# One core, a streaming encoder step: where the products with the expert weights are made, how many gathered rows run beside them, how the weights are put away, and how many v tiles are multiplied unsplit

## The chip, the core and the metric

The kernel runs on one core of one Trainium2 chip. The core has TensorE (PE, with the loading of its weights shown as PEld), VectorE (DVE), ScalarE (ACT), GpSimd (POOL), SyncE (SP, which here only issues transfers) and 16 DMA engines. The metric is the device time of one execution in microseconds (us). Before the change the median of 3 runs is 1786.55 us (1782.0 to 1789.22).

## The reference

One layer is computed for 384 tokens: 8 sequences of 16 tokens (the samples) and one prompt of 256 tokens. The layer has a modulation, an RWKV branch, a sparse attention branch, a mix, and then PEER, a layer with 16,384 experts. Only PEER is touched here:

```
q = (hb @ w_pq).reshape(PEER_BLOCK, PEER_HEADS, 2, PEER_DHALF)
s = jnp.einsum('nhpd,hpkd->nhpk', q, peer_keys)
s1, i1 = lax.top_k(s[:, :, 0], PEER_TOPK)
s2, i2 = lax.top_k(s[:, :, 1], PEER_TOPK)
...
sc, j = lax.top_k(cand, PEER_TOPK)
e = jnp.take_along_axis(cidx, j, axis=-1)
g = jax.nn.softmax(sc, axis=-1)
act = jax.nn.gelu(jnp.einsum('nhkd,nd->nhk', peer_u[e], hb))
out = jnp.einsum('nhk,nhkd->nd', (g * act), peer_v[e])
```

Each token picks 8 x 16 = 128 experts; an expert has a row u and a row v of 1024 numbers each. All in 32-bit floats.

## The kernel before

**Two ways to PEER.** The 128 sample tokens are done sparsely: 128 times, one picked expert of each token is gathered by an indirect DMA (one *row*: 128 partitions x 2048 numbers, 1 MB, u and v beside each other). VectorE forms the dot product with u (L1567), ScalarE takes the gelu and the weight (L1568, L1569), VectorE adds the scaled v to the sum (L1573). Three buffers hold such rows. The 256 prompt tokens are done densely: all 16,384 experts, in 128 tiles of 128 experts. For tile j, `dense_u` multiplies u with the tokens and takes the gelu, giving an activation tile of 128 experts x 256 tokens; this is multiplied by the matrix of routing weights, which is zero for experts not picked; `dense_v` multiplies the product with v and adds it to four PSUM banks (`bx`, `cp` for the first 128 tokens, two of `dx` for the second).

**Kept and late tiles.** Tiles 0 to 75 are *kept*: their activations stay in SBUF (G1 and G2) before the routing weights exist. Tiles 76 to 127 are *late*: their activations are computed later (`gA`) or put to HBM and fetched again (`gO`, `gB`).

**The stages.** (1) `dense_u` for the kept tiles, the first 36 unsplit. (2) The weights stage: `weights` goes over the 256 tokens in 64 steps of 4. A step makes two one-hot factors `oh` (L1384 on VectorE; L1432 on VectorE or L1436 and L1437 on ScalarE), multiplies them on TensorE into a PSUM tile p of 4 tokens x 128 tiles, multiplies the 76 kept columns into G1 and G2 (L1397, two instructions, 36 and 40 columns), and copies the 52 late columns to `wst` (L1398), which after 8 steps goes to HBM (L1400): the put-away weights. In odd steps ScalarE first copies the kept columns to `wg` (L1394, two buffers) and GpSimd makes the product; in even steps VectorE makes it straight from PSUM. After each step `ahead` is called: half of the times it runs a `dense_u` of a late tile, 31 in all, and it pulls rows at a rate `SR[1]`. (3) The v stage: 128 times a `dense_v`, kept and late tiles interleaved, with 21 more `dense_u` and rows at a rate `SR[2]`. Late weights are fetched for four tiles at a time (`Ws`, L1530) and multiplied on GpSimd (L1495). (4) The last two tiles and the residuals.

**Whole and split.** A number is cut into a high and a low part so that TensorE can use its faster mode (names ending in h and l: `wh`, `wl`, `Gh`, `Gl`). A *split* v tile costs a copy on ScalarE (L230) and a subtraction on VectorE (L234) for v and for G, and 12 matmuls of 512 columns. A *whole* tile needs none of that and 4 matmuls in full precision, which the trace shows as 8. `VN` says which are whole: the first three, and from the 9th to the 107th every n that VN divides.

**What sets the order.** The program is recorded in the order of the code, and a scheduler then orders each engine's instructions by a simulated time line; each engine runs its own list in order. Rows therefore run earlier or later than the place at which they were pulled. All plain transfers are issued by SP, in its order, each when its buffer is free; row gathers are issued by GpSimd in its own order, between its products. A row in the v stage is also held until a v tile five places before it is done (`pace`).

## Time and profile before

| | |
|---|---|
| median of 3 runs | 1786.55 us |
| profiled execution | 1789.7 us |
| its span | 1787.9 us |
| mean granted TensorE clock | 0.978 |
| PE, DVE, ACT, POOL busy, share of the span | 95%, 77%, 42%, 31% |
| HBM read, written | 403.23 MB, 31.30 MB |

The span is the time from the first to the last instruction; the execution's own time has 1.8 us around it. Busy times of an engine don't count waiting. A view "by stretches" gives, for a stretch of the span, the busy time of each engine with the number of instructions, the granted clock, the share of time in which the 16 DMA engines were busy, and the rate. The weights stage is the stretch from 1165 to 1305 us (ten of its 64 steps run some of their work before it), the v stage that from 1305 to 1758 us.

### The profile page before, as it was taken

What the parts mean: (1) busy time and instruction counts of PE and PEld (TensorE: products, weight loads), DVE (VectorE), ACT (ScalarE), POOL (GpSimd) and SP (SyncE); (2) the same over time, 40 slices, a digit from 0 to 9 for tenths busy, and PEclk for the clock granted to TensorE, in tenths of its full rate; (3) what the DMA queues carried; (4) which work ended last, traced back from release to release, by engine and by line L of the source; (5) the groups of instructions that cost most, each with busy time, mean ns of one, the idle gap of its engine ahead of it and who ended that gap; (6) DMA issues with size and microseconds to landing.
All of it is one profiled execution on the core that took longest, in us unless ns stands there. A gap on an engine that the chain in (4) does not pass through costs nothing.

```text
span 1787.9 us, 33229 instructions
## 1 busy us (share of the span) xinstructions
PE 1695.1 (95%) x12424; PEld 1414.2 (79%) x12424; DVE 1368.0 (77%) x2925; ACT 754.4 (42%) x1647; POOL 556.7 (31%) x648
## 2 busy tenths in 40 slices
PE   6999999999999998999999999999998989999998
PEld 4987788878888876998788789999976666666666
DVE  4538787777867765455999998899957877888787
ACT  4533333333243333334323365579833433334344
POOL 2423243333332320034032232333342324233232
PEclk8999899999999998999999999999999999999999
DMA  9443662454364365665498989975589989999995
GB/s 319 150 121 92 195 191 73 145 166 146 95 208 141 104 219 203 202 199 176 131 349 328 347 303 375 367 239 178 186 316 369 354 332 388 388 359 372 382 371 190
DMA packets 172537, 436.71 MB, mean 244 GB/s; under 512 B 46036, under 2 KB 86100, under 8 KB 155992
## 3 DMA queue, kind: packets, MB, share of 16 engines
q1 hardware_dynamic: 153944, 300.36, 49.9%
q0 software_dynamic: 18432, 134.23, 19.8%
q8 instruction: 98, 1.61, 0.4%
q14 instruction: 63, 0.52, 0.1%
HBM read 403.23 MB, written 31.30 MB: 243 GB/s over the span
## 4 chain that ended last, share of the span: by engine, by line
PE 55%; DVE 19%; DMA 13%; issue 7%; ACT 3%; POOL 2%; SPq 1%; DVEq 0%; POOLq 0%; ACTq 0%
PE mm L226 21%; PE fx L226 13%; PE dx L226 8%; PE cp L226 6%; PE bx L226 5%; DMA w<-in_pv 4%; DVE wl L234 3%; DMA w<-in_puT 3%; DVE raw L1567 3%; DVE acc L1573 2%; DMA raw<-in_puv,pe 2%; ACT wh L230 1%; DMA d<-MBp 1%; DMA NL<-d 1%; DMA w<-in_w_ada 1%
## 5 line engine op out<-in xcount | busy, mean ns | idle before, releaser
L234 DVE TENSOR_TENSOR wl<-w,wh 128x1024 fp32r<-128x1024 f32 (+1 forms) x280 | 352.8, 1265 | 121.2 <-ACT wh L230 80.2
L230 ACT ACTIVATE wh<-w 128x1024 fp32r<-128x1024 f32 (+1 forms) x288 | 301.1, 1052 | 195.0 <-PE mm L226 83.9
L1560 POOL DMA_INDIRECT raw<-in_puv,pe x128 | 169.3, 1323 | 438.8 <-PE dx L226 128.3
L226 PE MATMUL fx<-h2h,wl 128*128 128x256 f32 x736 | 210.5, 286 | 9.5 <-DVE wl L234 9.3
L226 PE MATMUL fx<-h2h,wh 128*128 128x256 f32 x736 | 212.9, 289 | 5.0 <-ACT wh L230 3.0
L226 PE MATMUL fx<-h2l,wh 128*128 128x256 f32 x736 | 207.6, 282 | 0.0
L1573 DVE SCALAR_TENSOR_TENSOR acc<-raw,dots,acc 128x1024 f32<-128x1024 f32 x127 | 166.5, 1311 | 18.3 <-ACT dots L1569 18.1
L1567 DVE SCALAR_TENSOR_TENSOR raw<-raw,sh 128x1024 f32<-128x1024 f32 x128 | 157.8, 1233 | 9.7 <-DMA raw<-in_puv,pe 9.6
L226 PEld LDWEIGHTS fx<-h2h,wl 128*128 128x128 f32 x736 | 138.4, 188 | 13.8 <-DVE wl L234 13.4
L226 PEld LDWEIGHTS fx<-h2h,wh 128*128 128x128 f32 x736 | 138.7, 188 | 9.3 <-ACT wh L230 5.0
L226 PEld LDWEIGHTS fx<-h2l,wh 128*128 128x128 f32 x736 | 138.7, 188 | 2.1 <-issue 1.6
L226 PE MATMUL fx<-h2f,w 128*128 128x256 f32 x576 | 131.1, 388 | 8.3 <-ACT G L1476 8.3
L226 PEld LDWEIGHTS fx<-h2f,w 128*128 128x128 f32 x576 | 110.6, 194 | 27.0 <-ACT G L1476 11.1
L226 PE MATMUL mm<-LTh,wh 128*128 128x384 f32 (+2 forms) x352 | 123.8, 352 | 2.0 <-ACT wh L230 1.4
L226 PE MATMUL mm<-LTl,wh 128*128 128x384 f32 (+2 forms) x352 | 123.1, 350 | 0.9 <-POOL LTl L481 0.9
L226 PE MATMUL mm<-LTh,wl 128*128 128x384 f32 (+2 forms) x352 | 122.4, 348 | 0.0
L226 PE MATMUL mm<-wh,LTh 128*128 128x256 f32 x336 | 101.0, 301 | 2.9 <-ACT qx L881 2.9
L226 PE MATMUL mm<-wl,LTh 128*128 128x256 f32 x336 | 100.2, 298 | 0.0
L226 PE MATMUL mm<-wh,LTl 128*128 128x256 f32 x336 | 99.4, 296 | 0.0
L1568 ACT ACTIVATE dots<-dots 128x1 f32<-128x1 f32 x128 | 25.5, 199 | 155.4 <-DVE raw L1567 154.8
L1397 POOL TENSOR_TENSOR G<-G,wg 128x144 f32<-128x144 f32 (+1 forms) x64 | 54.5, 875 | 92.8 <-ACT wg L1394 89.4
L226 PEld LDWEIGHTS mm<-LTh,wh 128*128 128x128 f32 (+2 forms) x352 | 66.5, 189 | 7.8 <-issue 2.8
(559 smaller groups left out, 4204.6 us busy)
## 6 DMA issues: line engine op xcount, KB each, us to landing
w<-in_puT SPq DMA_DIRECT2D x128, 512.0 KB
w<-in_pv SPq DMA_DIRECT2D x128, 512.0 KB
w<-in_w_in SPq DMA_DIRECT2D x70, 512.0 KB
w<-in_w_ada SPq DMA_DIRECT2D x48, 512.0 KB
cKT<-in_cKT SPq DMA_DIRECT2D x32, 256.0 KB
cV<-in_cV SPq DMA_DIRECT2D x32, 256.0 KB
w<-in_w_pq SPq DMA_DIRECT2D x16, 512.0 KB
d<-wst SPq DMA_DIRECT2D x8, 832.0 KB
```

What stands on the lines that cost most here:

```text
L226: return self.nc.tensor.matmul(out, l, r, start=start, stop=stop, skip_group_check=True, **kw)
L230: self.nc.scalar.activation(hi, src, AF.Copy)
L234: (self.nc.vector if eng == "v" else self.nc.gpsimd).tensor_tensor(lo, src, hi, op=OP.subtract)
L1397: (nc.vector if w is p else nc.gpsimd).tensor_tensor(g, g, w[:, :, c0:c1], op=OP.mult)
L1560: d = nc.gpsimd.indirect_dma_start(out=bass.AP(tensor=u.tensor, offset=u.offset, ap=[u.ap[0], [1, 2048]]), out_offset=None, in_=self.I["puv"],
L1567: nc.vector.scalar_tensor_tensor(u, u, 1.0, h2, op0=OP.mult, op1=OP.mult, accum_out=dot)
L1568: nc.scalar.activation(dot, dot, AF.Gelu_apprx_tanh)
L1573: nc.vector.scalar_tensor_tensor(acc, v, dot, acc, op0=OP.mult, op1=OP.add)
```

## The change

Four things change.

1. `EENG` goes from `'vg'` to `'g'`: all 64 steps copy the kept columns with ScalarE and multiply on GpSimd; VectorE makes none of these products. (128 products on GpSimd for 64, 64 copies for 32.)
2. `SR` goes from (0.5, 0.4, 0.69) to (0.5, 0.5, 0.63): in the weights stage 64 x 0.5 = 32 rows are pulled for 25.6, and fewer per v tile after it.
3. The put-away weights lie in HBM as 13 groups of 4 tiles x 128 partitions x 4 KB. A fetch of `Ws` reads 4 KB in one run per partition, where it read 8 runs of 512 B; the 8 writes go out in runs of 512 B, 13 per partition, where they had one run of 6.5 KB.
4. `VN` goes from 3 to 5: 20 v tiles from the 9th to the 107th are whole, where 33 were. With the first three that is 23 for 36; 105 are split for 92.

```
-SR, UR = (0.5, 0.4, 0.69), 0.5
+SR, UR = (0.5, 0.5, 0.63), 0.5
...
-UENG, VENG, GENG, VN = 'v', 'v', 'g', 3
+UENG, VENG, GENG, VN = 'v', 'v', 'g', 5
 SENG = 'gv'
-HENG, EENG, OB = 'va', 'vg', 3
+HENG, EENG, OB = 'va', 'g', 3
...
-                nc.sync.dma_start(self.Wd[(t0 + n) // 32], st)
+                nc.sync.dma_start(self.Wd[:, :, (t0 + n) // 32].rearrange("g p a -> p g a"), st.rearrange("p (g a) n -> p g (a n)", a=4))
...
-        self.nc.sync.dma_start(self.ws, self.Wd[:, :, j - NW:j - NW + 4].rearrange("c p a n -> p c a n"))
+        self.nc.sync.dma_start(self.ws.rearrange("p c a n -> p c (a n)"), self.Wd[(j - NW) // 4])
...
-        self.Wd = self.dt_([8, 128, 128 - NW, 32])
+        self.Wd = self.dt_([(128 - NW) // 4, 128, 8, 128])
```

The scheduler also orders the lists anew. GpSimd in the weights stage, just after the kept activations are complete, before the change (`raw` is a row, `G` the kept activations, `wg` the copied weights):

```order
L1397 TENSOR_TENSOR G_11240<-G_11240,wg_13305 128x4x36
L1397 TENSOR_TENSOR G_2286_11708<-G_2286_11708,wg_13305 128x4x40
L1560 DMA raw_15365<-in_puv,pe_2034_10447 128x2048
L1397 TENSOR_TENSOR G_11240<-G_11240,wg_13367 128x4x36
L1397 TENSOR_TENSOR G_2286_11708<-G_2286_11708,wg_13367 128x4x40
L1560 DMA raw_15394<-in_puv,pe_2034_10447 128x2048
L1397 TENSOR_TENSOR G_11240<-G_11240,wg_13442 128x4x36
L1397 TENSOR_TENSOR G_2286_11708<-G_2286_11708,wg_13442 128x4x40
```

and a stretch of the same stage with it:

```order
L1397 TENSOR_TENSOR G_11240<-G_11240,wg_13530 128x4x36
L1397 TENSOR_TENSOR G_2286_11708<-G_2286_11708,wg_13530 128x4x40
L1560 DMA raw_15317<-in_puv,pe_2034_10447 128x2048
L1397 TENSOR_TENSOR G_11240<-G_11240,wg_13583 128x4x36
L1397 TENSOR_TENSOR G_2286_11708<-G_2286_11708,wg_13583 128x4x40
L1560 DMA raw_15388<-in_puv,pe_2034_10447 128x2048
L1397 TENSOR_TENSOR G_11240<-G_11240,wg_13600 128x4x36
L1397 TENSOR_TENSOR G_2286_11708<-G_2286_11708,wg_13600 128x4x40
L1397 TENSOR_TENSOR G_11240<-G_11240,wg_13654 128x4x36
L1397 TENSOR_TENSOR G_2286_11708<-G_2286_11708,wg_13654 128x4x40
```

Behind the first full products (those of both G1 and G2) two row gathers stand among GpSimd's products before the change, and eight with it. On VectorE 52 rows' dot products (L1567) stand before the end of the weights stage before the change, and 58 with it, so 76 and 70 stand in the v stage.

TensorE at the end of the weights stage (`oh`: the product of a step; `fx`: a `dense_u`; `w,G`: the first whole v tiles), before the change:

```order
L226 MATMUL fx_15252<-h2h_11699,wh_15253 128x256
L226 MATMUL fx_15252<-h2l_11700,wh_15253 128x256
L226 MATMUL fx_15252<-h2h_11699,wl_15254 128x256
L226 MATMUL mm_15287<-oh_15284 128x128 x4
L226 MATMUL cp_15309<-oh_15302 128x128 x4
L226 MATMUL bx_15324<-w_15340,G_11240 128x512
```

and with it:

```order
L226 MATMUL mm_15185<-oh_15182 128x128 x4
L226 MATMUL bx_15202<-oh_15195 128x128 x4
L226 MATMUL mm_15256<-oh_15253 128x128 x4
L226 MATMUL cp_15273<-oh_15266 128x128 x4
L226 MATMUL mm_15327<-oh_15324 128x128 x4
L226 MATMUL bx_15344<-oh_15337 128x128 x4
L226 MATMUL mm_15398<-oh_15395 128x128 x4
L226 MATMUL fx_15561<-h2h_11699,wh_15562 128x256
L226 MATMUL fx_15561<-h2l_11700,wh_15562 128x256
L226 MATMUL bx_15437<-w_15446,G_11240 128x512
```

The 31 `dense_u` of the stage stand earlier: behind the last of them come nine steps, where two came before the change.

## The prediction

> **What bounds the kernel now.** I read the page's engine shares first (TensorE 95% of the span), then the view by stretches, then the groups and waits of the weights stage and of the v stage. The changes fall into these two.
>
> ```profile
> core 0: us, PE busy (x) PEld busy (x) DVE busy (x) ACT busy (x) POOL busy (x), PEclk, DMA share, GB/s
> 1165.00:1305.00 140.00, 137.76 (x1158) 135.06 (x1158) 132.70 (x201) 117.29 (x287) 49.05 (x57) 1.00 0.59 198
> 1305.00:1758.00 453.00, 428.82 (x1792) 302.56 (x1791) 351.98 (x419) 177.09 (x368) 150.57 (x128) 0.99 0.96 362
> ```
>
> In the weights stage TensorE is idle for 2.2 of 140 us: it sets the end, with VectorE (132.7) close behind, ScalarE at 117.3, GpSimd at 49.0 and the DMA engines at 0.59. In the v stage TensorE is idle for 24.2 of 453 us while the DMA engines are at 0.96, so two limits lie close together. TensorE's idle time there has names:
>
> ```profile
> PE bx L226 <- ACT wh L230: 10.2, 11, 1.6
> PE bx L226 <- DVE wl L234: 8.1, 12, 1.8
> PE fx L226 <- DVE wl L234: 4.3, 6, 1.3
> PE fx L226 <- ACT wh L230: 1.2, 1, 1.2
> ACT wh L230 <- DMA w<-in_pv: 21.3, 14, 3.4
> ACT wh L230 <- DMA w<-in_puT: 12.8, 8, 2.4
> DVE wl L234 <- ACT wh L230: 49.5, 39, 3.9
> ```
>
> The first four rows sum to 23.8 us: TensorE waits only for split weights, and those wait for ScalarE's copy, which waited 34.1 us for transfers. So DMA is the last cause of a part of these 24 us, not certainly of all.
>
> **The change part by part: the v stage.** First, 13 tiles become split. TensorE's time line around 1540 us (start, duration, instruction):
>
> ```profile
> 1535.72 0.39 PE L226 MATMUL bx<-wh,Gh 128*128 128x512 f32 x1
> ...
> 1538.47 0.28 PE L226 MATMUL fx<-h2h,wh 128*128 128x256 f32 x1
> ...
> 1541.31 1.02 PE L226 MATMUL bx<-w,G 128*128 128x512 f32 x2
> ...
> 1544.34 0.79 PE L226 MATMUL bx<-wh,Gh 128*128 128x512 f32 x1
> ...
> 1547.50 0.39 PE L226 MATMUL bx<-wh,Gh 128*128 128x512 f32 x1
> ```
>
> A split tile takes 1538.47 - 1535.72 = 2.75 us. A whole tile takes 1544.34 - 1541.31 = 3.03, and the split tile behind it 3.16 for 2.75, so a whole one costs 3.03 + 0.41 = 3.44. Thirteen conversions: 13 x 0.69 = 9.0 us less of TensorE. They add work on two others:
>
> ```profile
> L234 DVE TENSOR_TENSOR wl<-w,wh 128x1024 fp32r<-128x1024 f32 x104 | 131.5, 1274 | 50.6 <-ACT wh L230 49.5 <-PE dx L226 1.1
> L1573 DVE SCALAR_TENSOR_TENSOR acc<-raw,dots,acc 128x1024 f32<-128x1024 f32 x76 | 100.8, 1326 | 16.1 <-ACT dots L1569 15.9
> L1567 DVE SCALAR_TENSOR_TENSOR raw<-raw,sh 128x1024 f32<-128x1024 f32 x76 | 94.3, 1240 | 6.2 <-DMA raw<-in_puv,pe 6.1
> L234 DVE TENSOR_TENSOR Gl<-G,Gh 128x256 fp32r<-128x256 f32 x51 | 24.6, 484 | 13.9 <-PE dx L226 8.9 <-ACT dots L1568 3.1 <-ACT Gh L230 1.6
> L230 ACT ACTIVATE wh<-w 128x1024 fp32r<-128x1024 f32 x105 | 108.9, 1047 | 34.4 <-DMA w<-in_pv 21.3 <-DMA w<-in_puT 12.8
> L230 ACT ACTIVATE Gh<-G 128x256 fp32r<-128x256 f32 x51 | 21.0, 414 | 61.4 <-PE dx L226 59.5 <-DMA d<-wst 1.8
> ```
>
> VectorE gains 13 x (1.274 + 0.484) = 22.9 us and ScalarE 13 x (1.047 + 0.414) = 19.0. Six rows leave the stage (76 dot products become 70): VectorE loses 6 x (1.326 + 1.240) = 15.4. Net VectorE goes from 352.0 to 359.5 and ScalarE from 177.1 to about 196, both far below 435; this is hidden as totals, though each of the 13 tiles now has the two waits that only split tiles have.
>
> The six rows and the new layout take load off the DMA engines:
>
> ```profile
> q1 hardware_dynamic: 153944, 300.36, 49.9%
> q0 software_dynamic: 18432, 134.23, 19.8%
> Ws<-d SPq DMA_DIRECT2D x13, 512.0 KB
> ```
>
> Queue 0 carries the 128 rows: 0.198 x 1787.9 = 354 us of all 16 engines, 2.77 each, so six are 16.6 us. For the layout no row times a 512 B packet, so I estimate it. Queue 0's packets, nearly all 8 KB, moved 134.23 MB in 16 x 354 = 5664 engine-us, 23.7 KB per us. At that rate queue 1's 300.36 MB need 12,670 engine-us; it took 0.499 x 1787.9 x 16 = 14,270. The excess, 1,600 over 153,944 packets, is 10.4 ns a packet. The fetches of `Ws` go from 13 x 1024 packets to 13 x 128: 11,648 x 10.4 ns / 16 = 7.6 us less. From below it is 0 (the excess is due to other packets), from above twice as much; I take 7.6, as these are among the smaller packets.
>
> [...]
>
> The DMA engines were busy for 0.96 x 453 = 435 us; now 435 - 16.6 - 7.6 = 411. If the stage stays at 0.96 it takes 428 us: **25 less**. If TensorE is the limit and keeps its 24.2 us of idle time, it takes 428.8 - 9.0 + 24.2 = 444: **9 less**. I take the middle, **17 less**: part of the idle time came through transfers, part through the order on ScalarE and VectorE.
>
> **The weights stage.** TensorE's work is unchanged, so nothing shorter than 137.8 us is to be had here. The groups:
>
> ```profile
> L1397 DVE TENSOR_TENSOR G<-G,mm 128x160 f32<-128x160 f32 (+1 forms) x57 | 25.0, 481 | 3.0 <-PE mm L226 3.0
> L1397 POOL TENSOR_TENSOR G<-G,wg 128x144 f32<-128x144 f32 (+1 forms) x56 | 47.3, 869 | 86.2 <-ACT wg L1394 86.2
> L1394 ACT ACTIVATE wg<-cp 128x304 f32<-128x304 f32 x14 | 6.1, 438 | 0.0
> L1436 ACT ACTIVATE oh<-clate,pT 128x128 f32<-128x128 f32 x108 | 34.5, 399 | 2.6 <-PE mm L226 2.6
> L1437 ACT ACTIVATE oh<-oh 128x512 f32<-128x512 f32 x27 | 17.3, 641 | 0.1
> L1398 ACT ACTIVATE wst<-mm 128x208 f32<-128x208 f32 x29 | 15.9, 547 | 12.0 <-DVE G L1397 8.0 <-DMA d<-wst 3.9
> L226 PE MATMUL mm<-oh 128*128 128x128 f32 x224 | 29.6, 275 | 0.0
> ```
>
> VectorE loses 25.0 us of products and gains six rows' 15.4: 123. GpSimd gains 57 products of 0.869 and six gathers, at 1.72 us (next fence): 49.0 + 49.5 + 10.3 = 109. ScalarE gains some 29 copies of 0.438, 12.7 us, and six rows' two small activations: a group of the v stage has 0.289 for one of them, so at most 0.6 a row, 3.5 in all. That makes 133.5. Every total is below 137.8, but ScalarE, at 117 of 140 before, now stands within 5 us of TensorE, in strict order, with GpSimd behind it through two `wg` buffers.
>
> ```profile
> L1560 POOL DMA_INDIRECT raw<-in_puv,pe x1 | 1.7, 1723 | 5.1 <-DVE acc L1573 5.1
> L1569 ACT ACTIVATE dots<-dots,pg 128x1 f32<-128x1 f32 x76 | 21.9, 289 | 1.5
> ```
>
> The first row also shows what can be queued: that gather waited 5.1 us on GpSimd for a row buffer that VectorE frees. Eight gathers now stand among the products, and behind a waiting one wait the products, then `wg`, then ScalarE. Two `wg` buffers cover two steps, 2 x 140 / 54 = 5.2 us, so I cost this at nothing; without that cover it is up to 8 x 5.1 = 41 us.
>
> The order of the lists shows where that bites. With the change nine steps stand on TensorE behind the last `dense_u` of the stage, seven more than before. Such a step is 8 matmuls, 29.6 / 28 = 1.06 us on TensorE; on ScalarE it is a `wg` copy and a `wst` copy (0.438 + 0.547) and every second time a one-hot (4 x 34.5 / 108 + 0.641 = 1.92), 1.95 a step. So seven uncovered steps cost 7 x (1.95 - 1.06) = 6 us, and 1 us for the later last write of `wst`, whose eight transfers have 12,288 packets more (12,288 x 10.4 ns / 16 = 8 us, one eighth of it at the end; the others lie in a stage where the DMA engines are 0.41 idle). From below the cost is 0: the tail's one-hots may be ready early. From above ScalarE keeps all its 22.7 us of idle time beside 133.5 of work: 156, 16 more. I take **7 more**.
>
> Sum against the profiled execution: 1789.7 - 17 + 7 = 1779.7. The median of the runs stands 3.15 lower, and 1786.55 - 10 is 1776.5: I predict **1776 us**. All else is the same code and the tail from 1758 us on is left as it is.
>
> **The rivals.**
>
> *ScalarE and TensorE keep all that DMA gives.* The v stage is limited by TensorE and gains 9 only, the weights stage pays 7: 1784.5, no change. For it: DMA share 0.96 can go with TensorE at 428.8 of 453. Against it: 34.1 us of ScalarE's waits are for transfers.
>
> *GpSimd's products hold up VectorE* (the slower side). Its place is the weights stage: the products take 587 ns at the least and up to 2832, and VectorE's one-hots, 670 at the least, have a mean of 751 beside them:
>
> ```profile
> L1397 POOL TENSOR_TENSOR G<-G,wg x56: 587/664/2832, 1170.8 to 1303.8; 128x144 f32<-128x144 f32 x28, 128x160 f32<-128x160 f32 x28
> L1384 DVE TENSOR_TENSOR oh<-wA,wB x54: 670/681/2304, 1166.3 to 1297.6; 128x512 f32<-128x512 f32 x54
> L1384 DVE TENSOR_TENSOR oh<-wA,wB 128x512 f32<-128x512 f32 x54 | 39.2, 751 | 0.0
> ```
>
> If each of the 57 new products stops VectorE for its whole 0.869 us, VectorE has 123 + 49.5 = 172.5 us: the stage takes 35 us more with its 2.2 of idle time, and the kernel 1786.55 - 17 + 35 = 1804. It decides from 137.8 - 123 = 14.8 us on, 0.26 us a product; seen now are 54 x 0.081 = 4.4 us on the one-hots over 56 products, 0.08 each. The products that leave VectorE read one operand from PSUM; the rows that come read both from SBUF. [...]
>
> *All of the DMA relief arrives, and the weights stage costs nothing:* 1786.55 - 25 = 1761.5. For it: VectorE's load in the weights stage falls by 10 us, and total ScalarE work still fits. Against it: the nine steps at the end.
>
> **How the numbers follow.** The forecast has 0.40, with a range of its own from 1768 to 1784; no change 0.22; VectorE held up 0.15 (from 1790 to 1804); the full relief 0.23. Less than half a per cent, 8.9 us, cannot be told from no change, so faster is below 1777.6 and slower above 1795.5. Faster: six tenths of the forecast, 0.24, and the full relief, 0.23, together 0.47. Slower: most of the held-up case, 0.13, and 0.06 for a stage that costs ScalarE's full 16 us with a v stage that gains nothing: 0.19. Same: 0.34. The range goes from 1757, just below the full relief, to 1801, near the held-up case.
>
> **What would show it.** Right: 70 dot products in a v stage of 430 to 444 us, TensorE's idle time there below 20 us, DMA share at 0.96 or less; a weights stage of 143 to 152 us with TensorE idle in its last 15 us, waiting for `oh` or for PSUM that ScalarE frees. Wrong: a v stage within 5 us of 453 (then its limit is the latency from transfer to split weights, which 13 more split tiles make worse), or a weights stage over 160 us, or VectorE above 137 us of work in it, or GpSimd's products above 1 us each.

## The result, and the profile after

The changed kernel takes **1804.72 us** (median of 6 runs, 1799.46 to 1810.87) where the kernel before, run beside it, takes 1787.06 (6 runs, 1769.09 to 1793.82). The ratio is 1.0113, 95% interval 1.0086 to 1.014: slower. The forecast was 1776 us in a range from 1757 to 1801. The profiled execution, the longest of the six, took 1810.87 us with a span of 1809.1 and a mean granted clock of 0.979 (before: 1789.7, 1787.9, 0.978).

Here and below the **weights stage** goes from the last kept gelu on ScalarE to the first `dx` matmul of a whole v tile; *v and tail* is the rest of the span. (The prediction's window began some 8 us later and ended 2 us earlier.) The view by stretches, first of before, then of after; the columns are the length, then PE, PEld, DVE, ACT and POOL busy, the granted clock, the DMA share and GB/s:

```profile
1156.53:1307.25 150.72, 147.17 (x1220) 142.76 (x1219) 140.90 (x212) 124.79 (x306) 55.84 (x64) 1.00 0.60 203
1307.25:1787.90 480.65, 451.59 (x1893) 321.36 (x1891) 368.82 (x440) 185.78 (x379) 153.80 (x130) 0.99 0.94 351
```

```profile
1157.31:1336.61 179.30, 156.62 (x1222) 149.54 (x1221) 159.67 (x168) 137.38 (x350) 129.56 (x134) 0.96 0.64 207
1336.61:1809.10 472.49, 442.40 (x1943) 329.81 (x1941) 376.23 (x448) 197.87 (x392) 148.73 (x124) 0.99 0.91 343
```

All of the loss is in the weights stage: **28.6 us longer**, with 44 instructions fewer on VectorE but 18.8 us more of VectorE work. The rest is 8.2 us shorter, where the forecast had 17. VectorE's largest groups in the weights stage, before and after (instructions, busy us, mean ns, idle time before them):

```profile
L234 DVE TENSOR_TENSOR wl<-w,wh 128x1024 fp32r<-128x1024 f32 x33 | 43.5, 1323 | 5.9 <-ACT wh L230 5.5 <-ACT wst L1398 0.4
L1384 DVE TENSOR_TENSOR oh<-wA,wB 128x512 f32<-128x512 f32 x55 | 40.1, 754 | 0.0
L1397 DVE TENSOR_TENSOR G<-G,mm 128x160 f32<-128x160 f32 (+1 forms) x62 | 27.2, 481 | 3.0 <-PE mm L226 3.0
L1432 DVE TENSOR_TENSOR oh<-pT,dx 128x512 f32<-128x512 f32 x27 | 18.3, 677 | 0.0
L1573 DVE SCALAR_TENSOR_TENSOR acc<-raw,dots,acc 128x1024 f32<-128x1024 f32 x5 | 7.1, 1416 | 0.0
L1567 DVE SCALAR_TENSOR_TENSOR raw<-raw,sh 128x1024 f32<-128x1024 f32 x4 | 5.1, 1270 | 0.0
```

```profile
L1384 DVE TENSOR_TENSOR oh<-wA,wB 128x512 f32<-128x512 f32 x55 | 52.4, 974 | 3.1 <-ACT gO L1476 1.3 <-PE mm L226 1.0 <-ACT wst L1398 0.6
L234 DVE TENSOR_TENSOR wl<-w,wh 128x1024 fp32r<-128x1024 f32 x33 | 51.0, 1553 | 5.6 <-ACT wh L230 5.0 <-PE fx L226 0.6
L1432 DVE TENSOR_TENSOR oh<-pT,dx 128x512 f32<-128x512 f32 x27 | 18.2, 675 | 0.0
L1567 DVE SCALAR_TENSOR_TENSOR raw<-raw,sh 128x1024 f32<-128x1024 f32 x10 | 18.0, 1796 | 0.0
L1573 DVE SCALAR_TENSOR_TENSOR acc<-raw,dots,acc 128x1024 f32<-128x1024 f32 x11 | 15.9, 1443 | 0.0
```

The products (27.2 us) are gone, six rows came (a dot product L1567 and a sum L1573 each), and instructions that stayed got longer: the one-hots L1384 754 to 974 ns, the subtractions `wl` 1323 to 1553, the dot products 1270 to 1796. L1432 did not (677, 675). It reads an operand from PSUM (`dx` holds its iota); the others read both operands from SBUF. The sums L1573 read both from SBUF too and hardly moved as a group (1416, 1443): three of the five in before already ran beside a product of GpSimd (1508 ns on the mean, the other two 1277), and four of the eleven in after beside none (1274, the other seven 1540). So a group's mean depends on what runs beside it. The one-hots by themselves (least, median and longest ns), before and after:

```profile
L1384 DVE TENSOR_TENSOR oh<-wA,wB x55: 670/681/2304, 1163.6 to 1297.6; 128x512 f32<-128x512 f32 x55
L1384 DVE TENSOR_TENSOR oh<-wA,wB x55: 676/1047/4333, 1163.6 to 1325.1; 128x512 f32<-128x512 f32 x55
```

The least is the same. By the start and end times in the changed kernel's trace, 16 of these one-hots overlap no product of GpSimd (or by less than 50 ns) and take 676 to 693 ns; the 39 that overlap one have a mean of 1094. The time line of the changed kernel at one of its worst places, GpSimd and then VectorE:

```profile
1174.62 8.66 POOL L1397 TENSOR_TENSOR G<-G,wg 128x144 f32<-128x144 f32 x10
1191.97 2.40 POOL L1397 TENSOR_TENSOR G<-G,wg 128x144 f32<-128x144 f32 x4
```

```profile
1174.26 0.68 DVE L1432 TENSOR_TENSOR oh<-pT,dx 128x512 f32<-128x512 f32 x1
1174.86 4.33 DVE L1567 SCALAR_TENSOR_TENSOR raw<-raw,sh 128x1024 f32<-128x1024 f32 x1
1191.62 3.83 DVE L234 TENSOR_TENSOR wl<-w,wh 128x1024 fp32r<-128x1024 f32 x1
```

While GpSimd ran ten products back to back, a dot product (1.27 us on the mean before) took 4.33, as long as five of the products (0.87 each). The same happened to a subtraction beside a run of four products 17 us later, 3.83 us for 1.32.

### The profile page after: what moved, and what is told of

It is laid out like the page before. It is cut to its first block, busy times and chain, and to the rows that moved or that the text cites. A ratio compares the mean times of both kernels' runs of the same rounds, so it can differ in the third digit from the quotient of the medians.

```text
span 1809.1 us, 33476 instructions
## 1 busy us (share of the span) xinstructions
PE 1691.6 (94%) x12476; PEld 1426.8 (79%) x12476; DVE 1394.6 (77%) x2887; ACT 779.0 (43%) x1705; POOL 626.6 (35%) x712
## 3 DMA queue, kind: packets, MB, share of 16 engines
q1 hardware_dynamic: 154584, 300.36, 49.5%
q0 software_dynamic: 18432, 134.23, 19.6%
## 5 line engine op out<-in xcount | busy, mean ns | idle before, releaser
L234 DVE TENSOR_TENSOR wl<-w,wh 128x1024 fp32r<-128x1024 f32 (+1 forms) x293 | 380.1, 1302 | 114.9 <-ACT wh L230 69.9
L230 ACT ACTIVATE wh<-w 128x1024 fp32r<-128x1024 f32 (+1 forms) x301 | 314.9, 1051 | 163.9 <-PE mm L226 85.8
L1560 POOL DMA_INDIRECT raw<-in_puv,pe x128 | 175.2, 1368 | 426.2 <-PE dx L226 164.5
L226 PE MATMUL fx<-h2h,wl 128*128 128x256 f32 x736 | 214.2, 292 | 14.0 <-DVE wl L234 14.0
L1573 DVE SCALAR_TENSOR_TENSOR acc<-raw,dots,acc 128x1024 f32<-128x1024 f32 x127 | 167.8, 1321 | 6.6 <-ACT dots L1569 6.5
L1567 DVE SCALAR_TENSOR_TENSOR raw<-raw,sh 128x1024 f32<-128x1024 f32 x128 | 163.1, 1274 | 6.7 <-DMA raw<-in_puv,pe 6.7
L226 PEld LDWEIGHTS fx<-h2h,wl 128*128 128x128 f32 x736 | 141.4, 192 | 19.3 <-DVE wl L234 17.9
L226 PEld LDWEIGHTS fx<-h2h,wh 128*128 128x128 f32 x736 | 141.6, 192 | 12.9 <-ACT wh L230 8.5
L1397 POOL TENSOR_TENSOR G<-G,wg 128x144 f32<-128x144 f32 (+1 forms) x128 | 119.6, 968 | 43.1 <-ACT wg L1394 39.5
L1568 ACT ACTIVATE dots<-dots 128x1 f32<-128x1 f32 x128 | 25.6, 200 | 143.8 <-DVE raw L1567 143.4
```

The source lines that it names most:

```text
L226: return self.nc.tensor.matmul(out, l, r, start=start, stop=stop, skip_group_check=True, **kw)
L230: self.nc.scalar.activation(hi, src, AF.Copy)
L234: (self.nc.vector if eng == "v" else self.nc.gpsimd).tensor_tensor(lo, src, hi, op=OP.subtract)
L1397: (nc.vector if w is p else nc.gpsimd).tensor_tensor(g, g, w[:, :, c0:c1], op=OP.mult)
L1560: d = nc.gpsimd.indirect_dma_start(out=bass.AP(tensor=u.tensor, offset=u.offset, ap=[u.ap[0], [1, 2048]]), out_offset=None, in_=self.I["puv"],
L1567: nc.vector.scalar_tensor_tensor(u, u, 1.0, h2, op0=OP.mult, op1=OP.mult, accum_out=dot)
```

## The experiments

**How they are read.** One profile of each kernel is compared stage by stage, and the medians with before's own runs on the same chip. Six of the profiles share before's v stage (before, products alone, small reads, writes, ones, and layout, which differs in its fetches alone); their v and tail took 470.5 to 480.7 us, mean 475.5, so a single v stage is known to some 5 us, and before's profile is the longest of them. A profile is one execution, which can stand off its kernel's median: those of e15, e4 and e12 took 13.8, 10.6 and 7.4 us more than their medians, that of e5 8.9 less. What a v stage is said to cost is therefore checked by the medians too. Weights stages of like kernels agree within 1 us. The table puts all beside each other; the columns come from the view by stretches as above, idle is the length less PE's busy time, and the ratio is that of the medians to before with its interval.

| kernel | weights stage | VectorE in it | difference | v and tail | PE busy there | PE idle there | ratio |
|---|---|---|---|---|---|---|---|
| before | 150.7 | 140.9 | 9.8 | 480.7 | 451.6 | 29.1 | |
| rows alone (e5) | 165.8 | 157.3 | 8.5 | 462.4 | 443.0 | 19.4 | 1.0036 (1.0014 to 1.0057) |
| layout alone (e3) | 151.7 | 141.0 | 10.7 | 474.6 | 448.0 | 26.6 | 0.9996 (0.9974 to 1.0018) |
| every fifth tile whole alone (e4) | 151.3 | 141.0 | 10.3 | 486.5 | 447.8 | 38.7 | 1.0056 (1.0031 to 1.0081) |
| layout and fifth (e12) | 151.5 | 141.4 | 10.1 | 484.9 | 446.9 | 38.0 | 1.007 (1.0038 to 1.0101) |
| products alone (e2) | 158.2 | 143.9 | 14.2 | 477.0 | 450.1 | 26.8 | 1.0056 (1.0028 to 1.0084) |
| all but products (e1) | 166.3 | 154.8 | 11.5 | 464.3 | 438.9 | 25.4 | 1.0029 (1.0002 to 1.0055) |
| after | 179.3 | 159.7 | 19.6 | 472.5 | 442.4 | 30.1 | 1.0113 (1.0086 to 1.014) |
| after, third whole (e18) | 178.2 | 160.4 | 17.8 | 466.9 | 446.8 | 20.1 | 1.0118 (1.0083 to 1.0153) |
| all but products, idle reads (e7) | 165.5 | 153.5 | 12.0 | 467.4 | 438.9 | 28.5 | 1.0166 (1.0113 to 1.0219) |
| copies as after, products half on VectorE (e6) | 173.3 | 165.4 | 7.9 | 468.4 | 440.1 | 28.3 | 1.0111 (1.0045 to 1.0177) |
| before and small reads (e10) | 153.9 | 145.5 | 8.4 | 473.2 | 448.5 | 24.7 | 1.0018 (0.9999 to 1.0036) |
| before and writes (e11) | 151.4 | 140.4 | 11.0 | 470.5 | 445.9 | 24.6 | 1.0016 (1.0 to 1.0032) |
| before and products by ones (e13) | 168.4 | 161.3 | 7.2 | 477.2 | 448.5 | 28.7 | 1.0099 (1.0069 to 1.0129) |
| rows earlier (e14) | 162.7 | 152.1 | 10.6 | 468.9 | 448.2 | 20.7 | 1.0049 (1.0028 to 1.007) |
| fewer rows (e15) | 145.4 | 129.7 | 15.8 | 498.3 | 460.5 | 37.9 | 1.0069 (1.0043 to 1.0096) |
| every second whole (e16) | 151.4 | 142.3 | 9.1 | 479.4 | 457.2 | 22.2 | 1.004 (1.0016 to 1.0063) |
| second whole, fewer rows (e17) | 144.4 | 129.1 | 15.3 | 495.1 | 462.8 | 32.3 | 1.0079 (1.0051 to 1.0107) |

Against 475.5 for v and tail and 150.7 for the stage, the profiles add up to the medians within 3 us: ones, 17.7 + 1.7 = 19 us for a measured 18; rows, 15.1 - 13.1 = 2 for 5; fifth alone, 0.6 + 11 = 12 for 10.

**The change without the products, and the products alone.** The first undoes `EENG` in the changed kernel, the second does it in the kernel before.

```
-HENG, EENG, OB = 'va', 'g', 3
+HENG, EENG, OB = 'va', 'vg', 3      # e1: in the changed kernel
...
-HENG, EENG, OB = 'va', 'vg', 3
+HENG, EENG, OB = 'va', 'g', 3       # e2: in the kernel before
```

> The changed kernel with its products shared again (every second step's product on VectorE, straight from PSUM); rows, layout and v tiles as changed. Theory A (GpSimd's products and VectorE's instructions with two SBUF operands hold each other up in the weights stage): most of the stage's 30 us come back, 1774 to 1782 us, VectorE's one-hot (L1384) back from a mean of 974 ns to about 760. Theory B (ScalarE's copies and its order, with the uncovered steps at the end, set the stage): also faster, since 32 copies go, but L1384 changes little. Theory C (the six rows moved into the stage do it): it stays near 1800.

> The kernel before with one edit: all products on GpSimd behind ScalarE's copies; rows, layout and v tiles as before. Theories A and B: 20 to 33 us slower than before, 1807 to 1820 us. Theory C: within 8 us of before.

Measured: 1788.97 and 1794.98 us beside 1784.69 for before. Neither time is one that a theory gave: both kernels are slower than before by less than the whole loss. Most of it comes with the products (1.0113 with, 1.0029 without), and the other three parts don't gain anything either. Alone the products cost 7.5 us of stage though they take 27.2 us from VectorE: its work in the stage doesn't fall, it rises by 3.0. So 27.2 + 3.0 = 30.2 us came back as longer instructions, 0.49 us for each of the 62 products moved. VectorE's one-hots in the kernel with the products alone:

```profile
L1384 DVE TENSOR_TENSOR oh<-wA,wB 128x512 f32<-128x512 f32 x55 | 55.1, 1025 | 2.4 <-ACT gO L1476 1.8 <-PE mm L226 0.5
L1432 DVE TENSOR_TENSOR oh<-pT,dx 128x512 f32<-128x512 f32 x27 | 18.2, 676 | 0.0
```

**The rows alone.**

```
-SR, UR = (0.5, 0.4, 0.69), 0.5
+SR, UR = (0.5, 0.5, 0.63), 0.5
```

> The kernel before with one edit: rows pulled at 0.5 in the weights stage and 0.63 behind it. From the first four runs: the stage from the last kept gelu to the first v product on the dx banks grew from 150.7 to 166.3 us when the rows moved in without GpSimd's products, so I now hold VectorE's work there as the bound (140.9 us before; a row is 2.6). Theory D (the stage ends with VectorE's sum): stage 163 to 167 us, the v stage and the end 12 to 17 us shorter, total within 5 us of before. Theory E (the 15.6 us came from the layout's writes or the split v tiles): stage within 4 us of 150.7.

Measured: 1787.45 beside 1782.72. By stretches:

```profile
1148.65:1314.43 165.78, 152.97 (x1222) 145.63 (x1221) 157.33 (x232) 128.80 (x320) 65.13 (x70) 0.99 0.64 225
1314.43:1776.80 462.37, 442.97 (x1891) 318.87 (x1889) 354.90 (x422) 181.59 (x364) 144.53 (x124) 1.00 0.93 350
```

Six rows put 16.4 us of work on VectorE (six times a dot product and a sum) and the stage takes 15.1 us more; TensorE's work in it is the same code, and TensorE stands idle for 12.8 us of it where it did for 3.6. **VectorE, not TensorE, sets this stage.** What the v stage gives back is 18.3 us against before's profile, 13.1 against the mean of six, and 10.4 by the medians (15.1 less the 4.7 that the kernel lost).

**Only the copies.** In the changed kernel ScalarE still copies in every step, but VectorE makes the even steps' product from the copy:

```
-                (nc.vector if w is p else nc.gpsimd).tensor_tensor(g, g, w[:, :, c0:c1], op=OP.mult)
+                (nc.gpsimd if n // 4 % 2 else nc.vector).tensor_tensor(g, g, w[:, :, c0:c1], op=OP.mult)
```

> The changed kernel with ScalarE's copies in all 64 steps kept, but in every second step VectorE multiplies the copy instead of GpSimd. ScalarE's work is that of the changed kernel; GpSimd makes 64 products instead of 128. Theory B: no gain over the changed kernel, 1800 to 1808 us. Theory A: most of the loss goes, 1778 to 1788 us, though VectorE's products now read two SBUF operands themselves. Theory C: near 1800.

Measured: 1798.47 beside 1784.69, with four runs, and 10 us above the time that the theory of the products had; the stage 173.3 with ScalarE at 136.8 us, as in the changed kernel. VectorE's group, then its products one by one (least, median, longest) in before and here:

```profile
L1397 DVE TENSOR_TENSOR G<-G,wg 128x160 f32<-128x160 f32 (+1 forms) x63 | 35.7, 621 | 1.5 <-ACT wg L1394 1.5
```

```profile
L1397 DVE TENSOR_TENSOR G<-G,mm x62: 446/484/519, 1157.4 to 1301.8; 128x160 f32<-128x160 f32 x32, 128x144 f32<-128x144 f32 x30
L1397 DVE TENSOR_TENSOR G<-G,wg x63: 439/496/1875, 1153.4 to 1319.4; 128x160 f32<-128x160 f32 x32, 128x144 f32<-128x144 f32 x31
```

The mean is 621 ns where the product from PSUM took 481, but reading from SBUF isn't slower by itself: the 37 products that overlap none of GpSimd's have a mean of 479, the 26 that do one of 822. The copy made VectorE's product one more instruction with two SBUF operands. VectorE's work exceeds that of e1 by 10.6 us, the stage by 7.0. The difference between stage and VectorE is 7.9, among the lowest: beyond this the copies on ScalarE show no cost of their own.

**GpSimd work without any other change.** Four kernels add instructions to GpSimd and leave everything else. The first stands on e1, the others on the kernel before. The added work leaves the outputs as they are; it overwrites a constant that is no longer used, and in e13 multiplies G by one. Only the lines that make the added instructions are shown, without their loops and conditions; `dm` is the constant, `k` what is read, and the ones of e13 are filled in beforehand.

```
# e7, before the copy to wst, two in each even step, from a constant:
+                    nc.gpsimd.tensor_tensor(dm, k, k, op=OP.mult)
# e10, two in each even step, reading the wst slice just written (k):
+                    nc.gpsimd.tensor_tensor(dm, k, k, op=OP.mult)
# e11, two in each even step, after the wst copy, writing only:
+                    self.after(nc.gpsimd.memset(dm, 0.5), stc)
# e13, behind each product that VectorE makes, the same slice of G times ones:
+                    nc.gpsimd.tensor_tensor(g, g, self.ident[:, :c1 - c0].unsqueeze(1).to_broadcast([128, 4, c1 - c0]), op=OP.mult)
```

> The first kernel of this call with two extra GpSimd multiplications in every second step, of 4 x 31 numbers a partition, from a constant in SBUF into a constant that is not used any more; nobody waits for them. They add work to GpSimd alone, with no copy on ScalarE and nothing in the chain of a step. Theory A: VectorE's one-hot and weight subtractions are stretched again, mean of L1384 above 850 ns, and the time goes to 1790 to 1803 us. Theories B and C: within 6 us of the first kernel of this call.

> The kernel before with two extra GpSimd multiplications of 4 x 31 numbers in every even step, tied to the step: they read the just copied put-away weights in SBUF and write a constant that is not used any more. VectorE keeps its products, ScalarE its copies, rows as before. Theory A (VectorE and GpSimd stop each other when both read SBUF): VectorE's L1384 goes from a mean of 754 ns to 850 to 1000, its work in the stage from 140.9 to 155 us or more, the stage from 150.7 to 162 to 175 us. If GpSimd's products cost only by ScalarE's copies and the order: stage within 5 us of before.

> As the run with reads, but the two GpSimd instructions fill the same constant with a number: they write and read nothing. If it is GpSimd's reading that stops VectorE: L1384 stays below 790 ns and the stage within 5 us of 150.7. If any GpSimd work does it: as in the run with reads, in proportion to its busy time.

> The kernel before (products of the even steps stay on VectorE), and behind each of these products GpSimd multiplies the same slice of G in place by ones, so that GpSimd has the real products' shapes, strides and places in its queue without a copy wg and without taking anything from VectorE. The result is not touched. Theory 'GpSimd instructions of this shape hold up VectorE': GpSimd goes from 55.8 to about 105 us in the weights stage, VectorE's one-hots (L1384, mean 751 ns before, 1025 ns with the products moved) go to about 1000, VectorE's work in the stage rises from 140.9 by 25 to 35 us, and the stage takes 20 to 30 us longer: 1803 to 1813. Rival 'only copies and queueing on ScalarE cost, GpSimd's reads stretch VectorE as little as the small ones did': L1384 stays below 800, VectorE gains 3 to 6 us, and the kernel stays within 5 us of before.

*e7* (1812.34 beside 1784.69) can't be used for the question: the added products depend on nothing, and the scheduler put them before the stage, between the row gathers. There GpSimd was busy for 36 of 40 us, and TensorE for only 10.1 of the second 20:

```profile
1040.00:1060.00 20.00, 19.78 (x156) 19.57 (x155) 19.87 (x24) 15.15 (x37) 18.30 (x21) 0.92 0.66 234
1060.00:1080.00 20.00, 10.12 (x80) 9.51 (x79) 10.06 (x12) 4.29 (x11) 17.85 (x28) 0.85 0.52 178
```

In that stretch a dot product waited 9.9 us for its row, and TensorE 9.4 us for a subtraction behind it in VectorE's list. The last kept gelu came at 1175.66 us, 22 us later than in e1, and the weights stage itself took 165.5, as in e1 (166.3). Here idle work ahead of the gathers in GpSimd's list delayed what waited for the rows (in the second 20 us of that stretch TensorE was busy for 19.8 us in e1); it says nothing on VectorE's instructions in the weights stage.

*e10 and e11* are tied to their steps. 64 small products (44.5 us) put 4.6 us on VectorE's work, where the theory had 14 or more; 64 writes (12.9 us) put none. Neither is clear of no change in time (1785.74 and 1782.72 beside 1782.72). The writes are a small load, for which the rate of the small products would give 1.3 us, no more than the spread of like kernels (140.9 to 142.3); but the groups' means didn't rise either (one-hots 749 ns, subtractions 1302; 754 and 1323 before), and taken one by one, the 6 one-hots and 8 subtractions that overlap a write and no product have means of 680 and 1218 ns, those that overlap neither 680 and 1212.

*e13* has the real products' shapes and strides. (Their second operand is a row of ones.) It takes 1800.5 us beside 1782.52, **18 us more, without taking anything from or giving anything to another engine**. The group that was added on GpSimd, and VectorE's groups beside it (its L1385, L1398 and L1435 are L1384, L1397 and L1432):

```profile
L1400 POOL TENSOR_TENSOR G<-G,cfirst 128x160 f32<-128x160 f32 (+1 forms) x62 | 52.1, 863 | 38.7 <-DVE G L1398 38.7
```

```profile
L1385 DVE TENSOR_TENSOR oh<-wA,wB 128x512 f32<-128x512 f32 x55 | 51.9, 967 | 0.0
L234 DVE TENSOR_TENSOR wl<-w,wh 128x1024 fp32r<-128x1024 f32 x34 | 50.0, 1475 | 8.3 <-ACT wh L230 8.3
L1398 DVE TENSOR_TENSOR G<-G,mm 128x160 f32<-128x160 f32 (+1 forms) x62 | 27.1, 478 | 0.0
L1435 DVE TENSOR_TENSOR oh<-pT,dx 128x512 f32<-128x512 f32 x27 | 18.2, 674 | 0.0
```

L1384 goes to 967 ns as in the changed kernel, and the two that read PSUM stay at 478 and 674. VectorE's work in the stage rises by 161.25 - 140.90 = 20.4 us over 62 products, 0.33 us each, and the stage by 17.7. The theory of the products holding up VectorE had 25 to 35 us and 20 to 30 of stage: right in kind and a third too dear.

**The layout and the v tiles.** Each alone in the kernel before, and both together; then every second tile whole, and the changed kernel with every third.

```
# e3: the three lines on Wd, as in the change
# e4:
-UENG, VENG, GENG, VN = 'v', 'v', 'g', 3
+UENG, VENG, GENG, VN = 'v', 'v', 'g', 5
# e12: both     # e16: VN = 2     # e18: the changed kernel with VN = 3
```

> The kernel before with only the layout of the put-away weights changed. My sum had 7.6 us less DMA in the v stage and 1 us more for the writes: if DMA bounds the v stage and a 512 B packet costs more than its bytes, about -5 us. Rival 'a 512 B run already goes at line rate': 0 to +1.

> The kernel before with only every fifth, not third, v tile whole. Together with the layout it was 1.007 of before. Theory 'split tiles wait for a chain transfer, ScalarE, VectorE, and thirteen more of them cost more than their 9.0 us of TensorE': slower by 5 to 12 us, TensorE's idle time in the v stage above 35 us. Rival 'the layout is what cost': within 2 us of before.

> The kernel before with the new layout of the put-away weights and every fifth v tile whole; products and rows as before. By my sum of the v stage, 9 us less TensorE work and 7.6 us less DMA work: 1772 to 1782 us, 3 to 12 us faster. If the 13 more split tiles cost their waits on ScalarE and VectorE: within 3 us of before or slower.

> The kernel before with every second v tile whole: 16 tiles whole that were split. Theory 'a split tile costs its chain of waits': what 13 more split tiles cost (10 us, 0.75 each) comes back, 16 x 0.75 = 12 us: about 1771. Rival 'TensorE's work counts': 16 x 0.69 = 11 us more, 1793. Rival 'the chain costs only when VectorE is over about 0.8 of the v stage': no change within 4 us.

> The changed kernel with every third v tile whole again (rows, products and layout stay). If thirteen split tiles cost as alone, 10 us less than the changed kernel: about 1793, ratio 1.006. If they cost nothing once the rows have left the v stage, as the run without the products suggests (the v stages of e1 and e5 differ by 2 us): 1801, ratio 1.010.

Measured: layout 1782.47, fifth 1792.19, beside 1782.52; both 1792.62 beside 1782.72; second 1788.56 and the changed kernel with third 1802.14, beside 1782.6. The layout does nothing that can be measured, alone or in e12, which is 9.9 us slower as e4 is 9.7 slower, where the sum of the v stage had 3 to 12 faster. Thirteen more split tiles cost 10 us alone; in the changed kernel they cost nothing that can be seen (1.0113, and 1.0118 with every third whole). The v and tail of e4 by stretches, and then its largest waits of TensorE there (the first number is the sum in us, the second how often):

```profile
1314.51:1801.00 486.49, 447.77 (x1945) 333.79 (x1943) 389.40 (x466) 201.61 (x405) 153.28 (x130) 0.98 0.92 347
```

```profile
PE bx L226 <- ACT wh L230: 18.6, 13, 3.0
PE bx L226 <- DVE wl L234: 5.3, 10, 1.2
PE fx L226 <- ACT wh L230: 4.9, 4, 2.2
```

By the table's means, whose profiles differ by up to 10 us, the thirteen tiles take 1.4 us from TensorE's work where the rows stay (448.8 for the six kernels with every third tile whole, 447.3 for e4 and e12) and 4.8 where they have moved (444.9 for e5 and e18; 440.1 for e1, e6, e7 and after), not 9.0 (the mean granted clock of that stretch is 0.98 in e4 and e12 and 0.99 or 1.00 in the six, so part of it may have gone into slower matmuls). They add 11.6 us of idle time (26.7 to 38.4), or 8.3 (19.8 to 28.1). In all the stretch gets 10.2 us longer where the rows stay (9.1 by the medians of e4 and e12 less what their stages grew), and 3.5 where they have moved (464.6 to 468.2). The waits of a v stage's first matmuls for ScalarE's copy (`bx <- ACT wh`) go with the number of split tiles: 4.5 us with every second whole, 10.2 in before and 7.9 in e5, 18.6 in e4, and 12.7 and 13.0 in e1 and after, which have the same tiles as e4. ScalarE itself waits less for transfers in e4 (25.8 us, 41.7 before), and more for TensorE, ahead of its copies of G:

```profile
L230 ACT ACTIVATE Gh<-G 128x256 fp32r<-128x256 f32 x63 | 26.0, 416 | 82.3 <-PE dx L226 80.3 <-DMA d<-wst 2.0
```

Before, that row had 53 copies and 59.5 us of such waits. ScalarE's list is in order, so a copy `wh` stands behind a `Gh` that waits for TensorE. That this is the chain which makes `wh` late is argued from these rows and wasn't tried by itself. Every second tile whole isn't better than every third, and the 1771 us of the theory of waits didn't come: TensorE's work rises by 8.4 us (457.2) and the waits don't fall as far; of the three numbers tried, three is the best.

**The version that would follow.** If rows cost VectorE's time in the weights stage, they should go elsewhere: earlier, or into the v stage.

```
# e14: S0, PH = 20, 4 and SR = (0.5, 0.4, 0.65)
# e15: SR = (0.5, 0.33, 0.73)
# e17: e15 with VN = 2
```

> The kernel before with the first gathered rows started ten tiles earlier in the dense u stage (S0 20, not 30; SR[2] 0.65), so that about five rows leave the v stage without entering the weights stage. Theory 'the weights stage is set by VectorE, the v stage by DMA': the weights stage stays at 151 us, the v stage is 5 x 2.77 = 14 us shorter, and the u stage, where VectorE is at 0.74 and DMA at 0.68, hides the rows: about 1770. Rival 'a row costs its VectorE time wherever it is put': the u stage takes 5 x 2.6 = 13 us more, and nothing changes: 1783 to 1787.

> The kernel before with SR = (0.5, 0.33, 0.73): some four gathered rows less in the weights stage, as many more in the v stage. Theory 'VectorE sets the weights stage': it is shorter by 2.6 us a row (about 10), the v stage longer by 2.8 to 3 us a row, as in the run that moved six rows the other way: no change, 1778 to 1787. Rival 'the weights stage is set by TensorE': it stays at 150 us and the kernel takes 11 us more, 1793.

> Both: every second v tile whole and four rows moved from the weights stage into the v stage, where VectorE loses 28 us and gets 10. Theory 'split tiles cost by VectorE's load, and rows theirs by VectorE in the weights stage': the sum of the two single runs or a little better, 1765 to 1778. Rival 'DMA or TensorE bounds the v stage': 1790 or more.

Measured: 1790.85 beside 1782.52; 1792.57 and 1796.58 beside 1782.6. All three are slower, and the gains that were hoped for in e14 and e17 didn't come; the times of the rivals in e15 (1793) and e17 (1790 or more), which had TensorE or DMA as the limit, did. The stage of e15 got shorter all the same, which its rival denied. In e14 no dot product came earlier (48 before the stage, as in before); four went from the v stage into the weights stage, which took 12.0 us more. In e15 the stage fell by 5.3 us only, since the other limit was reached:

```profile
1160.84:1306.28 145.44, 144.57 (x1214) 141.29 (x1213) 129.65 (x198) 119.97 (x296) 50.64 (x62) 1.00 0.53 186
```

TensorE is busy for 144.6 of 145.4 us, with VectorE at 129.7. So TensorE's floor of this stage is some 145 us, VectorE needs its work plus 7 to 12, and the kernel before stands 6 us above TensorE's floor. The v stage paid for five more rows 22.8 us by the profile against the mean, and 15.3 by the medians (10.0 that the kernel lost, and 5.3 that the stage gained). No kernel that was run is faster than the kernel before.

## Why the prediction was wrong

The forecast was 10 us faster; the kernel is 17.7 us slower by the medians, outside the stated range. Two of the signs that the prediction named for being wrong came: a weights stage over 160 us (179.3) and VectorE above 137 us of work in it (159.7).

**The weights stage: +7 predicted, +28.6 measured.** The step that failed is VectorE's total, "VectorE loses 25.0 us of products and gains six rows' 15.4: 123", and with it "Every total is below 137.8". The 25.0 us were counted off in full, and what GpSimd's products do to VectorE's other instructions was put at nothing and left to a rival. In the stage as measured here VectorE goes from 140.9 to 159.7, in three terms:

- *Six rows*: 16.4 us in e5, for 15.4. This size was right. The prediction counted them as covered by the total below TensorE's; in e5, where the products stay, they cost 15.1 us of stage.
- *The products*: 27.0 us off, for 25.0 in the prediction's shorter window. Right too.
- *What came back*: 159.7 - (157.3 - 27.0) = 29.4 us of stretching over 62 moved products, 0.47 us each, against nothing in the sum.

That is 16.4 - 27.0 + 29.4 = 18.8 us. The second half of the step is the bound. The sum took the busiest engine, TensorE, as the limit and the second busiest, VectorE at 132.7 of 140, as a total that fits below it. But VectorE's list is strictly in order, and its work plus 7 to 12 us is the stage in all kernels but those with the products moved and those with few rows. This bound alone would not have turned the forecast, since without the stretching VectorE's work falls; with the stretching that work goes above TensorE's and sets the stage. The other 9.8 us of the 28.6 are the end of the stage, below.

The rival named the mechanism and the point from which it decides, 0.26 us a product; it priced a whole product, 0.869. That its 1804 us stands beside the measured 1804.72 is luck: it had 49.5 us of stretching, 20 too many, and a v stage 17 us shorter, 9 to 14 too many. The row that spoke for it, 0.08 us on the one-hots beside 56 products, was read as if it would stay so with the double number. It was too small for another reason too: it looked at one group, and the subtractions and dot products stretch as well. The chance of 0.15 was too low.

What was held up went with the operands: in the changed kernel the instructions with two SBUF inputs were longer where they overlapped GpSimd's products than where they did not (1094 and 680 ns on the mean for the one-hots, 1644 and 1212 for the subtractions, 2046 and 1211 for the dot products), the two kinds with a PSUM operand stayed as they were (675 ns in the changed kernel, 478 in e13; 677 and 481 before), and writes cost nothing that shows (e11, 140.4 us of VectorE's work for 140.9). The rival's price, a whole product each time, was its author's assumption and isn't borne out on the average: 0.33 to 0.49 us per product of 0.86 to 1.00 (e13, after, e2), and 0.10 us per us for small spread reads (e10). Why a product that was moved costs more than one that was only added wasn't tried.

**The end of the weights stage** was one term that was nearly right in size: 7 us for the uncovered steps. The difference between the stage and VectorE's work is 19.6 us in the changed kernel, 9.8 before, so 9.8 us more. ScalarE, TensorE and the stretch of the changed kernel's last 20 us:

```profile
1317.27 0.42 ACT L1394 ACTIVATE wg<-bx 128x304 f32<-128x304 f32 x1 [0.29 <-POOL G L1397]
1318.86 0.42 ACT L1394 ACTIVATE wg<-mm 128x304 f32<-128x304 f32 x1 [0.64 <-POOL G L1397]
1319.18 1.27 ACT L1436 ACTIVATE oh<-clate,pT 128x128 f32<-128x128 f32 x4
1320.35 1.04 ACT L230 ACTIVATE wh<-w 128x1024 fp32r<-128x1024 f32 x1
1321.30 0.40 ACT L1394 ACTIVATE wg<-cp 128x304 f32<-128x304 f32 x1
1321.60 0.62 ACT L1437 ACTIVATE oh<-oh 128x512 f32<-128x512 f32 x1
1322.40 0.52 ACT L1398 ACTIVATE wst<-mm 128x208 f32<-128x208 f32 x1 [0.18 <-DMA d<-wst]
```

```profile
1318.47 1.13 PE L226 MATMUL cp<-oh 128*128 128x128 f32 x8
1322.97 2.07 PE L226 MATMUL mm<-oh 128*128 128x128 f32 x8 [3.37 <-ACT wst L1398]
1324.84 1.91 PE L226 MATMUL bx<-oh 128*128 128x128 f32 x8
```

```profile
1317.00:1337.00 20.00, 14.88 (x63) 10.99 (x64) 7.74 (x9) 11.58 (x28) 12.21 (x17) 0.83 0.42 127
```

TensorE waited 3.37 us for PSUM that the `wst` copies free, and these stood in ScalarE's list behind one-hots, a `wh` copy and `wg` copies. Within that gap ScalarE stood idle for 0.18 us only, so its own load, which the prediction had as the cause, is most of it. Its waits for `wg` buffers that GpSimd frees, for which the prediction held two buffers to be cover enough, come just before the gap and add up to 0.93 us in these lines. After that gap the granted clock was low (0.83 on the mean of the 20 us) and a step's eight matmuls took 2.07 us for 1.13, for which the sum had no term; on the two steps shown that is 3.98 - 2.26 = 1.7 us.

**The v stage: -17 predicted, -8.2 measured by the two profiles, and -3.0 against the mean of six.** The direction was right, two of its three terms were not.

- *Rows, 16.6 us of DMA*: the right order of size. The v stage gave back 18.3 against before's profile, 10.9 between the means (475.5, and 464.6 for e5 and e18), 10.4 by the medians.
- *Layout, 7.6 us*: nothing (0.9996). The estimate of 10.4 ns a packet came from the excess of a whole queue and put it all down to packets, with no row for a 512 B packet. The bound from below was the measured one.
- *Thirteen tiles, 9.0 us less TensorE*: TensorE's work fell by 1.4 to 4.8 us, not 9.0, so the 0.69 a tile read from one pair of tiles did not come, and its idle time rose by 8 to 12. The prediction had the last in its list of what would show it wrong (the waits of split tiles), but in no term. The middle between a DMA limit and a TensorE limit left out what split tiles wait for, which by the rows of e4 is their copies' turn in ScalarE's list.

**What the end would be by these terms:** 28.6 of weights stage, and v and tail between -3.0 and -8.2, is 20 to 26 us; the medians say 17.7, the ratio 20, and the profiled execution was 6.2 us above its median.

**Still open.** The v and tail of the changed kernel took 472.5 us, the three others with the same code there (e1, e6, e7) 464.3 to 468.4. Its TensorE was busy 3.5 us longer than in e1 and idle 4.7 us longer; whether this is the spread between executions (its profile was the longest of six runs) or what the longer weights stage leaves behind wasn't tried. And the parts don't simply add: rows and fifth alone cost 5 and 10 us, together with the layout 4.

## What to carry to other kernels

Where two engines are each busy for over nine tenths of a stage (here TensorE for 147.2 and VectorE for 140.9 of 150.7 us), count a change against both: the second one, with its waits, can be the bound, and then what is moved onto it can cost nearly its full time whatever the first one does (15.1 us for 16.4 here). Work that went from VectorE to GpSimd wasn't gone from VectorE here, whose instructions with two SBUF operands ran at that time: 27.2 us of products left it and 30.2 came back (e2). Price such a move by how long these take where they overlap GpSimd's products and where they don't (1094 and 680 ns for the one-hots here), in all groups and not in one, or leave an operand in PSUM, where nothing was stretched here (677 and 674 ns, 481 and 478, before and in e13). A tile that swaps TensorE work for a chain of copies on other engines is worth only what is left when its waits are taken off (thirteen took 1.4 to 4.8 us from TensorE's work here and added 8.3 to 11.6 of idle time), and these are seen in TensorE's idle rows, not in its busy time.

## What the runs showed of the hardware

- VectorE's one-hots (128x512), with both inputs in SBUF, stretched beside GpSimd products that read SBUF: 754 to 967 ns on the mean with 62 products of 0.86 us added (e13). Where they overlapped none they took 676 to 693 ns in the changed kernel. The two groups with one input in PSUM didn't stretch (677 and 674; 481 and 478, before and in e13). Beside GpSimd instructions that only write, the one-hots didn't either (680 ns, six of them, e11).
- Such an instruction was held up by several products in a row: a dot product of 1.27 us (the mean before) took 4.33 in the changed kernel, beside ten back to back. The average is far below that, 0.33 to 0.49 us a product (e13, after, e2).
- VectorE's product with both operands in SBUF took as long as the one with an operand in PSUM where it overlapped none of GpSimd's products (479 ns in e6, 481 before), and 822 ns where it did (e6): copying the PSUM operand out first exposed it to them.
- After 3.37 us without a matmul (to 1322.97 us) TensorE's next step in the changed kernel took 2.07 us, not 1.13, with a granted clock of 0.50 up to 1328 us and a mean of 0.83 in those 20 us. Behind a gap of 4.91 us (to 1181.81 us) and one of 2.06 us (to 1249.17) in the same stage, matmuls of 256 columns soon took 0.41 us, not 0.28, for some 3 us, at a granted clock of 0.50; behind one of 2.78 us (to 1213.52) they didn't (0.28 us, clock 1.00). So the length of the last gap doesn't decide it alone; what does was not shown.
- Runs of 512 B and of 4 KB for 13 fetches of 512 KB each gave the same time of the kernel (e3, 0.9996, 0.9974 to 1.0018).
